# Dealing a gated linear recurrence and windowed attention out to four engines in a written order, with the first rows of the output projection among them

## The chip, the cores and the metric

The kernel runs on one core of a Trainium2 chip. Time is device microseconds of one execution, the median of several runs. The engines named below are TensorE (PE, with its weight loads as PEld), VectorE (DVE), ScalarE (ACT), GpSimd (POOL) and SyncE (SP), which here only starts DMAs. Each engine works through its own instructions in order and waits on semaphores for the others.

## The reference

One layer of a decoder trunk on 1024 tokens of width 1024. The normed input is projected to 30 columns of 128. They feed three mixers: HGRN2, a gated linear recurrence with 4 heads of 128; attention over three dilated windows, 4 heads of 64, combined by their softmax denominators; and RWKV-7. Their outputs, side by side, go through an output projection; a gated MLP with a short convolution and a per-layer embedding follow.

```python
z = rmsnorm(h, norm_mix_g[l]) @ w_in[l]
o_a = hgrn2_mix(a_q, a_f, a_i, a_g, lbs[l], hgrn_gnorm_g[l])   # this stage
o_b = dilated_window_mix(b_q, b_k, b_v)                        # this stage
o_c, v_first = rwkv7_mix(c_in, ...)                            # done before it
h = h + concatenate([o_a, o_b, o_c], -1) @ w_out[l]            # the stage behind it
h = h + conv_glu_ffn(rmsnorm(h, norm_ffn_g[l]), ...)
gate = sigmoid(rmsnorm(h, norm_ple_g[l]) @ ple_gate[l])
h = h + gate * (p[l] @ ple_proj[l])
# hgrn2, per head: S_t = diag(f_t) S_{t-1} + (1 - f_t) i_t^T, o_t = S_t^T q_t, then
# o * rsqrt(mean(o*o) + eps) * gnorm_g * silu(g)
```

## The kernel before

Tiles hold 128 rows (a column of the projection, or 128 features) by T = 1024 tokens, in two halves of HT = 512. A projection product is done in split precision: a weight is cut into a high part `whi` and a low part `wlo`, an input into `xh` and `xl`, and three matmuls of 128x512 stand for one (lines 130, 132, 134). ACT casts `whi` (line 106), DVE or POOL subtracts to get `wlo` (line 108). The raw weights `wraw` have two buffers.

The kernel runs in stages: input norm, projection and RWKV-7 (0 to about 434 us of the profile), the stage with HGRN2 and attention (about 434 to 646), the output projection (to about 730), the MLP and the rest. The change is in the third part of `phase_mix`. There four generators are interleaved, each a stream of steps that end in `yield`:

- A does HGRN heads 0 and 2, B heads 1 and 3 (`hgrn_head`). A head loads `f` and `q` (tiles `zl`), makes the key `hk` and `qt`, and goes through one step with key-query products `hsc` at line 1002 and seven steps at line 1023. A step copies `hsc` into the score tile `hS` under a mask (line 1025), multiplies `hk` (1026, on POOL and DVE by turns) and `qt` (1028), makes the next level of decays `hT` (1033) and the next packed key `ks` (ACT, 1013). Then come transposes (`vt`, with copies `hV`, `hkt` on ACT), the chunk states `hkv` and `hst`, the output `hpo` and its copy `ho`, and a norm: square `hsq` on ACT, sum `hss` on DVE, power `hrs` on POOL, multiply `ho` on DVE (1100), transposes `vt` on PE (1106).
- C does attention for two head pairs p, each over query blocks qb 0 to 9 (`swa`): scores `swq` (1167), a masked copy with a row minimum `lg` on DVE (1174), the exponential on ACT (1176), transposes `swt` (1190) with copies `pT`, values `swo` (1203) with copies `ob`, and at the end denominators `swd` and the division. A step of C does scores of qb, values of qb-2 and transposes of qb-1 together.
- F projects the three columns of `w_in` that were left over (`project_late`), a half of 24 matmuls `zp` per step; the result is scaled by `rstd` on DVE (306), goes through a sigmoid on ACT (472) and a multiply (474) into `zst`, and is stored to memory as a column `z`.

`interleave` calls the streams by the letters of `order`: 36 rounds with one step of A each, from round 6 one of B, one of C in 23 of them, one of F in the odd rounds up to 13. This is the order in which the code is written; the order on each engine is then made by the tile scheduler, from its own cost model and priorities. PSUM has a pool of four banks (`mx`) for the small products and two double banks (`dp`) shared by the scores `swq` and the dense products `dp`.

Of the kernel before, what the change touches and what calls it, by code (L numbers as in the profile page):

```python
# [10 lines left out]
F32 = mybir.dt.float32  # L11
# [7 lines left out]
P = 128  # L19
# [48 lines left out]
def interleave(order, streams):  # L68

    live = dict(streams)  # L70
    while live:
        for s in order:
            if s in live and next(live[s], STOP) is STOP:
                del live[s]
# [5 lines left out]
class Trunk:  # L80
# [227 lines left out]
    def phase_mix(self):  # L308
        nc, tc = self.nc, self.tc
        self.mix_norm()  # L310
        with tc.tile_pool(name="slots", bufs=1) as slots:
            self.slots, self.NSLOT = slots, 8
            self.rwkv()
        self.O, self.done = None, []
        for p in (0, 1):
            self.o_split(6 + p)
        with tc.tile_pool(name="hg", bufs=1) as slots, tc.tile_pool(name="sw", bufs=1) as sp:
            self.slots, self.NSLOT = slots, 11
            self.hgrn_setup()
            self.sp = sp  # L320
            self.swmask = sp.tile([P, T], F32, name="swmask")
            nc.scalar.dma_start(self.swmask, self.a["swm"])
            A = chain(self.hgrn_head(0), self.hgrn_head(2))
            B = chain(self.hgrn_head(1), self.hgrn_head(3))
            order = []
            for r in range(36):
                order += "C" * (r in self.TURNS) + "A" + "B" * (r > 5) + "F" * (r % 2 and r < 14)
            interleave(order, {"A": A, "B": B, "C": self.swa(sp), "F": self.project_late(self.rest)})

    TURNS = [i * 33 // 22 for i in range(23)]  # L330

    def mix_norm(self):

# [140 lines left out]
            self.nc.vector.tensor_tensor(dst, dst, src, ALU.mult)  # L474

    def project_late(self, js):


        nc = self.nc
        for j in js:  # L480
            w = self.load_w(self.a["w_in"][j])
            t = self.keep.tile([P, T], F32, tag="zst", name=self.nm("zst"), bufs=2)
            d = self.zpool.tile([P, T], F32, tag=f"z{j}", name=f"z{j}")
            kind = (j - 8) % 4 if j < 24 else 2
            turn = j < 24 and kind < 3
            for hf in (0, 1):
                ps = self.mxp.tile([P, HT], F32, tag="mx", name=self.nm("zp"))
                self.dense({hf: ps}, w, self.X, ND, halves=(hf,))
                dst = slice((hf ^ turn) * HT, ((hf ^ turn) + 1) * HT)
                r = self.R[:, hf * HT:(hf + 1) * HT]  # L490
                self.finish(kind, t[:, dst], *((ps[:, ::-1], r[:, ::-1]) if turn and hf else (ps, r)))
                nc.sync.dma_start(d[:, dst], t[:, dst])
                if hf:
                    self.z[j] = d
                yield
        self.O = self.xall()
        for k in self.done:
            self.o_split(k)
# [472 lines left out]
    def hgrn_head(self, h):  # L971
# [71 lines left out]
        for hf in (0, 1):  # L1043
            pt = mxp.tile([P, HT], F32, tag="mx", name=self.nm("vt"))
            for c in range(4):
                nc.tensor.transpose(pt[:, c * P:(c + 1) * P], vc[:, hf * HT + c * P:hf * HT + (c + 1) * P], self.ident)
            nc.scalar.copy(V[:, hf * HT:(hf + 1) * HT], pt)
        kt = self.slot("hkt")
        for hf in (0, 1):
            pt = mxp.tile([P, HT], F32, tag="mx", name=self.nm("vt"))  # L1050
# [46 lines left out]
        rs = spool.tile([P, 8], F32, tag="hrs", name=self.nm("hrs"))  # L1097
        nc.gpsimd.tensor_tensor(rs, ss, self.mhalf[:, :8], ALU.pow)
        o3 = o.rearrange("p (c v) -> p c v", v=P)
        nc.vector.tensor_tensor(o3, o3, rs.unsqueeze(2).broadcast_to([P, 8, P]), ALU.mult)  # L1100
        yield
        for hf in (0, 1):
# [9 lines left out]

    def swa(self, sp):

        pend, fin, load = [], None, self.swa_load(sp, 0)
        yield
        for p in (0, 1):
            d = load
            self.swa_values_in(d)
            for qb in range(10):  # L1120
                if fin:
                    self.swa_out(*fin)
                    fin = None
                if qb < 8:
                    cur = self.swa_scores(sp, d, qb)
                if qb > 1:
                    fin = self.swa_values(sp, d, *pend.pop(0))
                if 0 < qb < 9:
                    pend[-1:] = [self.swa_turn(sp, *pend[-1])]
                if qb < 8:  # L1130
                    pend.append((qb, *cur))
                if qb == 7 and p == 0:
                    load = self.swa_load(sp, 1)
                yield
        self.swa_out(*fin)

    def swa_load(self, sp, p):
        d = {"p": p}
        for i, n in enumerate("qkv"):
            d[n] = self.zload(24 + 3 * p + i, lambda n: sp.tile([P, T], F32, tag="sslot", name=self.nm(n), bufs=4),  # L1140
                              self.nc.gpsimd)
        return d

    def swa_values_in(self, d):
        nc, vc = self.nc, d["v"]
        V = self.sp.tile([P, T], F32, tag="sslot", name=self.nm("sV"), bufs=4)
        for hf in (0, 1):
            pt = self.mxp.tile([P, HT], F32, tag="mx", name=self.nm("vt"))
            for c in range(4):
                nc.tensor.transpose(pt[:, c * P:(c + 1) * P], vc[:, hf * HT + c * P:hf * HT + (c + 1) * P], self.ident)  # L1150
            nc.scalar.copy(V[:, hf * HT:(hf + 1) * HT], pt)
        d["V"] = V.rearrange("p (b c) -> p b c", c=P)

# [74 lines left out]
    def phase_out(self, hp, x0, emb):  # L1228


        nc = self.nc
        self.h = [hp.tile([P, T], F32, name=f"h{k}") for k in range(ND)]
        self.hd = [[self.zpool.tile([P, HT], F32, tag=f"hd{k}_{hf}", name=f"hd{k}_{hf}") for hf in (0, 1)] for k in range(ND)]
        for k in range(ND):
            nc.scalar.dma_start(self.h[k], self.a["xT"][k])
        acc = hp.tile([P, HT], F32, name="acc")

        def rows(m, halves, hooks={}):
            w = self.load_w(self.a["w_out"][m])
            ps = self.dps.tile([P, T], F32, tag="dp", name=self.nm("dp"))  # L1240
            self.dense([ps[:, :HT], ps[:, HT:]], w, self.O, (6, 7, 0, 1, 4, 2, 3, 5), halves, hooks)
            for g in halves:
                u = self.h[m][:, g * HT:(g + 1) * HT]
                nc.vector.tensor_tensor(u, u, ps[:, g * HT:(g + 1) * HT], ALU.add)
                nc.scalar.dma_start(self.hd[m][g], u)

        for m in range(ND):
            rows(m, (0, 1) if m < 2 else (0,))
            self.sq_acc(acc, self.h[m][:, :HT], m == 0)
        r = {}  # L1250

        def factor(i):
            if i == 0:
                r[0] = self.rstd_sums(acc, 1.0 / 1024, EPS, self.mxp.tile([P, 4], F32, tag="mx", name=self.nm("ps_ss")))
            else:
                r[1] = self.rstd_spread(r[0], self.mxp.tile([P, HT], F32, tag="mx", name=self.nm("ps_ss")))

        with self.tc.manual_schedule(engines={mybir.EngineType.PE}):
            rows(2, (1,), {0: lambda: factor(0), 3: lambda: factor(1)})
        pb = r[1]  # L1260
        x0.close()
        self.TX = {}
        for i, n in enumerate(("p1", "p2")):
            self.TX[n] = [[self.tile16(8 * i + 2 * k + c, F32R) for c in (0, 1)] for k in range(4)]
        self.ped = [self.zpool.tile([P, T], F32, tag=f"pe{m}", name=f"pe{m}") for m in range(ND)]
        pwp = emb.enter_context(self.pool("pw"))
        px, pw = [], []
        parts = [(px, self.pxp, "pT", 0), (pw, pwp, "ple_proj", 0), (px, self.pxp, "pT", 1), (pw, pwp, "ple_proj", 1)]
        norm = self.ffn_norm(0, pb)
        for m in range(3, ND):  # L1270
            rows(m, (1,))
            for _ in range(2):
                next(norm, None)
            if parts:
                self.pe_load(pwp, *parts.pop(0))
        for m in range(ND):
            self.sq_acc(acc, self.h[m][:, HT:], m == 0)
# [575 lines left out]
```

## Time and profile before

| | us |
|---|---|
| median of 3 runs (1493.87 to 1499.34) | 1497.36 |
| the profiled execution | 1496.24 |
| its span | 1494.5 |
| PE busy | 1445.1 (97%) |
| DVE busy | 1097.8 (73%) |
| ACT busy | 634.5 (42%) |
| POOL busy | 446.6 (30%) |

The mean granted clock of PE is 0.989 over the span. Times within the profile are from the span's start. A matmul's end is modelled and neighbours overlap, so the distance between two starts is the better price of one. A row with a wait says which engine waited at which line, and for what; "idle before" in a group is the idle time of its engine just ahead of its instructions.

### The profile page before, as it was taken

What the parts mean: (1) busy time and instruction counts of PE and PEld (TensorE: products, weight loads), DVE (VectorE), ACT (ScalarE), POOL (GpSimd) and SP (SyncE); (2) the same over time, 40 slices, a digit from 0 to 9 for tenths busy, and PEclk for the clock granted to TensorE, in tenths of its full rate; (3) what the DMA queues carried; (4) which work ended last, traced back from release to release, by engine and by line L of the source; (5) the groups of instructions that cost most, each with busy time, mean ns of one, the idle gap of its engine ahead of it and who ended that gap; (6) DMA issues with size and microseconds to landing.
All of it is one profiled execution on the core that took longest, in us unless ns stands there. A gap on an engine that the chain in (4) does not pass through costs nothing.

```text
span 1494.5 us, 20176 instructions
## 1 busy us (share of the span) xinstructions
PE 1445.1 (97%) x7416; PEld 1199.0 (80%) x7416; DVE 1097.8 (73%) x1650; ACT 634.5 (42%) x1121; POOL 446.6 (30%) x362
## 2 busy tenths in 40 slices
PE   8999999999989889999999999999999999999996
PEld 7888997888977677778878888888888888888775
DVE  7666455585648668736788888888888799777684
ACT  6531343213425635425454444444444444455542
POOL 3232432313412122112144554444554000002343
PEclk9999999999999989999999999999999999999998
DMA  6123112232152111165333333333332883351443
GB/s 219 58 92 99 43 56 72 72 99 63 43 179 74 42 73 57 43 229 194 127 110 98 103 106 106 106 106 106 106 106 81 313 298 97 105 164 42 139 157 106
DMA packets 79874, 167.83 MB, mean 112 GB/s; under 512 B 20064, under 2 KB 22240, under 8 KB 79776
## 3 DMA queue, kind: packets, MB, share of 16 engines
q1 hardware_dynamic: 65424, 145.44, 29.8%
q10 hardware_dynamic: 13264, 17.04, 3.4%
q0 software_dynamic: 1088, 4.06, 0.8%
q8 instruction: 58, 0.95, 0.3%
q14 instruction: 40, 0.33, 0.1%
HBM read 120.12 MB, written 46.40 MB: 111 GB/s over the span
## 4 chain that ended last, share of the span: by engine, by line
PE 84%; DVE 6%; issue 4%; POOL 2%; DMA 2%; ACT 1%; DVEq 0%; POOLq 0%; ACTq 0%; SPq 0%
PE bg L1325 16%; PE bv L1325 12%; PE dp L130 8%; PE dp L134 8%; PE dp L132 8%; PE bg L1626 7%; PE bv L1626 7%; PE hsc L1023 2%; DMA zl<-z 1%; PE swq L1167 1%; PE swo L1203 1%; POOL wlo L108 1%; PE bv L130 1%; PE bv L132 1%; PE swt L1190 1%
## 5 line engine op out<-in xcount | busy, mean ns | idle before, releaser
L130 PE MATMUL dp<-xh,whi 128*128 128x512 f32 x560 | 202.7, 406 | 1.1 <-ACT xh L374 1.1
L134 PE MATMUL dp<-xh,wlo 128*128 128x512 f32 x560 | 194.4, 391 | 2.0 <-POOL wlo L108 1.1
L132 PE MATMUL dp<-xl,whi 128*128 128x512 f32 x560 | 194.5, 391 | 0.4 <-DVE xl L375 0.3
L108 POOL TENSOR_TENSOR wlo<-raw,whi 128x512 fp32r<-128x512 f32 x84 | 138.0, 1662 | 77.8 <-ACT whi L106 77.8
L108 POOL TENSOR_TENSOR wlo<-wraw,whi 128x512 fp32r<-128x512 f32 x64 | 88.0, 1379 | 233.2 <-ACT whi L106 203.9
L1325 PE MATMUL bg<-t,whi 128*128 128x512 f32 x352 | 132.7, 389 | 0.0
L106 ACT CAST whi<-wraw 128x512 fp32r<-128x512 f32 x120 | 72.1, 617 | 132.7 <-PE dp L132 94.4
L134 PEld LDWEIGHTS dp<-xh,wlo 128*128 128x128 f32 x560 | 105.0, 188 | 25.0 <-POOL wlo L108 1.5
L130 PEld LDWEIGHTS dp<-xh,whi 128*128 128x128 f32 x560 | 104.5, 188 | 23.6 <-issue 3.8
L132 PEld LDWEIGHTS dp<-xl,whi 128*128 128x128 f32 x560 | 105.2, 188 | 21.8 <-DVE xl L375 1.4
L108 POOL TENSOR_TENSOR wlo<-s,whi 128x512 fp32r<-128x512 f32 x44 | 65.9, 1498 | 159.5 <-ACT whi L106 147.3
L1626 PE MATMUL bg<-t,whi 128*128 128x512 f32 x308 | 95.0, 389 | 0.0
L1626 PE MATMUL bv<-t,whi 128*128 128x512 f32 x308 | 94.8, 389 | 0.0
L106 ACT CAST whi<-raw 128x512 fp32r<-128x512 f32 x88 | 52.6, 619 | 97.4 <-PE bv L1325 49.0
L106 ACT CAST whi<-s 128x512 fp32r<-128x512 f32 x66 | 38.9, 620 | 120.7 <-PE bg L1325 113.3
L1325 PEld LDWEIGHTS bg<-t,whi 128*128 128x128 f32 x352 | 66.0, 188 | 13.6
L175 POOL TENSOR_TENSOR rst<-rst,mhalf 128x4 f32<-128x4 f32 (+1 forms) x9 | 9.8, 1088 | 223.4 <-DVE rst L173 223.4
L108 DVE TENSOR_TENSOR wlo<-wraw,whi 128x512 fp32r<-128x512 f32 x56 | 48.2, 863 | 34.8 <-ACT whi L106 32.4
L1622 ACT CAST t<-t 128x512 fp32r<-128x512 f32 x77 | 47.8, 622 | 47.8 <-PE bv L1626 34.8
L1626 PEld LDWEIGHTS bv<-t,whi 128*128 128x128 f32 x308 | 57.8, 188 | 12.1
L1626 PEld LDWEIGHTS bg<-t,whi 128*128 128x128 f32 x308 | 57.7, 188 | 12.0
L1325 PE MATMUL bg<-t,wlo 128*128 128x512 f32 x176 | 67.2, 389 | 0.0
(429 smaller groups left out, 3660.9 us busy)
## 6 DMA issues: line engine op xcount, KB each, us to landing
raw<-in_ffn_up_dram SPq DMA_DIRECT2D x44, 512.0 KB, 3.7
wraw<-in_w_in_dram SPq DMA_DIRECT2D x29, 512.0 KB, 3.6
z<-zst SPq DMA_DIRECT2D x19, 512.0 KB, 2.9
gb<-ct SPq DMA_DIRECT2D x33, 256.0 KB, 2.0
t<-gb SPq DMA_DIRECT2D x33, 256.0 KB, 2.8
t<-gt SPq DMA_DIRECT2D x33, 256.0 KB, 2.7
zl<-z SPq DMA_DIRECT2D x16, 512.0 KB, 3.5
wraw<-in_ple_gate_dram SPq DMA_DIRECT2D x16, 512.0 KB, 3.6
```

Source lines behind the costliest of these rows:

```text
L106: nc.scalar.copy(hi, src)
L108: eng.tensor_tensor(lo, src, hi.bitcast(F32), ALU.subtract)
L130: nc.tensor.matmul(ps[hf], wh, xh[hf], start=first, stop=False)
L132: nc.tensor.matmul(ps[hf], wh, xl[hf], start=False, stop=False)
L134: nc.tensor.matmul(ps[hf], wl, xh[hf], start=False, stop=last)
L1023: nc.tensor.matmul(sc[:, c, :], ks[:, c * P:(c + 1) * P], view(qt, c * P, [2 * n, 64 // n], [HT + n, 2], [1, n]), start=True, stop=True)
L1167: nc.tensor.matmul(pq[h][:, b:b + w], d["q"][hs, qb * P:nk], d["k"][hs, b:b + w], start=True, stop=True)
L1190: nc.tensor.transpose(pt[:, kb * P:(kb + 1) * P], lg[:, b + kb * P:b + (kb + 1) * P], self.ident)
L1203: nc.tensor.matmul(po[hs, :], d["V"][:, kb, hs], pT[h][:, kb * P:(kb + 1) * P], start=kb == 0, stop=kb == qb)
L1325: nc.tensor.matmul(ps, w[part == 2][:, s], X[k][part == 1], start=start and k == part == 0, stop=k == 3 and part == 2, skip_group_check=no ...
L1622: nc.scalar.copy(xh, x)
L1626: nc.tensor.matmul(ps[m], wt[part == 2][:, m * P:(m + 1) * P], (xh, xl)[part == 1], start=k == part == 0, stop=k == NK - 1 and part == 2)
```

## The change

It has five parts.

1. The streams run under `manual_schedule` for PE, DVE, ACT and POOL: on these four engines the instructions stand as the code is written. SP is still put in order by the scheduler. The letters come from `mix_order`: 39 rounds; a table gives each step its PE time in arbitrary units, and a step of C is dealt to a round when the sum so far is below the round's share. F's seven steps stand in rounds 0, 1, 3, 5, 7, 9 and 10, so that two halves of 24 products run back to back at the start.
2. A new stream W does the first five of eight products (k = 6, 7, 0, 1, 4) of the output projection's rows m = 0 and 1, in rounds 33 to 38; `rows` then adds the last three.
3. A step of C becomes three (scores; values; transposes), and two more yields in a head put the sum `hss` with the power `hrs`, the multiply of `ho`, and the transposes into three rounds.
4. The attention loads no longer share four slots: each has a tag of its own. For the second pair, q goes to a buffer of another pool and k to the place of the first pair's v, both through SP's queue after qb 5; v goes to the place of the first q through POOL's queue after qb 7.
5. `project_late` loads each next weight one column ahead and splits it right behind the second half of the column before.

```diff
+            late = self.project_late(self.rest)
+            E = mybir.EngineType
+            with tc.manual_schedule(engines={E.PE, E.DVE, E.Activation, E.Pool}):
+                interleave(self.mix_order(), {"A": A, "B": B, "C": self.swa(sp), "F": late, "W": self.out_steps()})
+    def mix_order(self):
+        head = [0, 0, 16] + [8] * 7 + [8, 8, 14, 30, 0, 0, 8]
...
+        late = (0, 1, 3, 5, 7, 9, 10)
+        per = (2 * sum(pairs) + sum(swa) + 48 * 6) / 36
...
+            while swa and done < per * (r + 1):
+                done += swa.pop(0)
+                n += 1
+            order += "A" * (r < 33) + "C" * (n // 2) + "B" * (r > 5) + "C" * (n - n // 2) + "F" * (r in late)
+            order += "W" * {33: 1, 35: 1, 36: 3, 37: 3, 38: 3}.get(r, 0)
...
+    def out_steps(self):
+        raws = [self.load_raw(self.a["w_out"][m]) for m in (0, 1)]
+        yield
+        for m in (0, 1):
+            w = self.split_w(raws[m])
+            ps = self.dps.tile([P, T], F32, tag="dp", name=self.nm("dp"))
+            self.part[m] = w, ps
+            for k in self.OUT_KS[:5]:
+                self.mm3([ps[:, :HT], ps[:, HT:]], w(k), self.O[k], k == 6, False)
+                yield
...
+            if more:
+                raw = self.load_raw(self.a["w_in"][js[n + 1]])
...
                 if hf:
                     self.z[j] = d
+                    if more:
+                        w = self.split_w(raw)
                 yield
...
         nc.gpsimd.tensor_tensor(rs, ss, self.mhalf[:, :8], ALU.pow)
         o3 = o.rearrange("p (c v) -> p c v", v=P)
+        yield
         nc.vector.tensor_tensor(o3, o3, rs.unsqueeze(2).broadcast_to([P, 8, P]), ALU.mult)
         yield
...
                 if qb < 8:
                     cur = self.swa_scores(sp, d, qb)
+                yield
                 if qb > 1:
                     fin = self.swa_values(sp, d, *pend.pop(0))
+                if qb == 1:
+                    self.swa_values_in(d)
+                yield
                 if 0 < qb < 9:
                     pend[-1:] = [self.swa_turn(sp, *pend[-1])]
                 if qb < 8:
                     pend.append((qb, *cur))
-                if qb == 7 and p == 0:
-                    load = self.swa_load(sp, 1)
+                if p == 0 and qb == 5:
+                    self.swa_load(ds[1], self.keep, "q", "oc", 2, self.nc.sync)
+                    self.swa_load(ds[1], sp, "k", "sc", 1, self.nc.sync)
+                if p == 0 and qb == 7:
+                    self.swa_load(ds[1], sp, "v", "sa")
                 yield
...
+            if m in self.part:
+                w, ps = self.part.pop(m)
+                for k in self.OUT_KS[5:]:
+                    self.mm3([ps[:, :HT], ps[:, HT:]], w(k), self.O[k], False, k == 5)
```

Where the order on the engines changes, two places. First PE at the end of a half of the late projection, before the change. Names carry a number for each buffer written; a row is an instruction, or several alike.

```order
1698 L134 MATMUL zp_3905<-xh_119,wlo_3901 128x512
1699 L1203 MATMUL swo_3944<-pT_3861,sV_3704 64x128
1700 L1203 MATMUL swo_3944<-pT_3866,sV_3704 64x128
...
1703 L1190 MATMUL swt_3951<-cst,lg_3850 128x128 x3
1704 L1190 MATMUL swt_3957<-cst,lg_3853 128x128 x3
1705 L1023 MATMUL hsc_3962<-qt_3732,ks_3890 128x128 x4
1706 L1167 MATMUL swq_3978<-zl_3696,zl_3694 128x512
1707 L1167 MATMUL swq_3979<-zl_3696,zl_3694 128x512
...
```

With the change, at the end of the third half (the second is `zp_3753`):

```order
1686 L134 MATMUL zp_3854<-xh_119,wlo_3786 128x512
1687 L1070 MATMUL hsc_3883<-qt_3751,ks_3847 128x128 x4
1688 L1246 MATMUL swt_3895<-cst,lg_3810 128x128
1689 L1246 MATMUL swt_3899<-cst,lg_3813 128x128
1690 L1223 MATMUL swq_3902<-zl_3708,zl_3706 128x384
1691 L1223 MATMUL swq_3903<-zl_3708,zl_3706 128x384
1692 L1070 MATMUL hsc_3912<-qt_3751,ks_3891 128x128 x4
1693 L130 MATMUL zp_3923<-xh_89,whi_3780 128x512
```

Behind a half stood two lots of values, two of transposes, an `hsc` and the scores; now an `hsc`, two single transposes and the scores, and then the next `hsc`.

DVE at the same places, before:

```order
489 L1033 TENSOR_TENSOR hT_4071<-hT_4071 128x8
490 L306 TENSOR_TENSOR zp_3905<-zp_3905,rstd 128x512
491 L1025 COPY_PREDICATED hS_3773<-cmask,hsc_3962 128x512
492 L474 TENSOR_TENSOR zst_3903<-zst_3903,zp_3905 128x512
493 L1028 TENSOR_TENSOR qt_3732<-qt_3732,hT_3775 128x2x32x8
494 L1026 TENSOR_TENSOR hk_3729<-hk_3729,hT_3775 128x2x8x32
495 L1174 ISA lg_3984,sden_3977<-swq_3978,swmask 128x640
496 L1174 ISA sden_3977 128x1
```

and with the change:

```order
455 L1080 TENSOR_TENSOR hT_3790<-zl_3712 128x512
456 L306 TENSOR_TENSOR zp_3854<-zp_3854,rstd 128x512
457 L513 TENSOR_TENSOR zst_3852<-zst_3852,zp_3854 128x512
458 L1072 COPY_PREDICATED hS_3788<-cmask,hsc_3883 128x512
459 L1073 TENSOR_TENSOR hk_3748<-hk_3748,hT_3790 128x2x128x2
460 L1075 TENSOR_TENSOR qt_3751<-qt_3751,hT_3790 128x2x128x2
461 L1080 TENSOR_TENSOR hT_3790<-hT_3790 128x256
```

Before, the mask copy of `hsc` stands between the scaling of `zp` and its multiply into `zst`; now both stand ahead of the mask copy, and `hk` and `qt` behind it, with the levels `hT` each behind its `qt`. Lines of the new file stand 47 to 56 rows further down here: 1072 is 1025, 1075 is 1028, 1080 is 1033, 513 is 474, 1230 is 1174.

Second, the loads of the second attention pair. Before, all three are on POOL: q, `zl_4394`, early (row 121), k and v, `zl_4396` and `zl_4398`, here:

```order
133 L157 TENSOR_TENSOR xl_4507<-oc_1640,xh_4506 128x512
134 L108 TENSOR_TENSOR wlo_5630<-wraw_5622,whi_5628 128x512
135 L157 TENSOR_TENSOR xl_4509<-oc_3267,xh_4508 128x512
136 L502 DMA zl_4396<-z_3663 128x1024
137 L502 DMA zl_4398<-z_3745 128x1024
138 L1098 TENSOR_TENSOR hrs_4480<-hss_4477,mhalf 128x8
139 L1026 TENSOR_TENSOR hk_4024<-hk_4024,hT_4071 128x2x4x64
```

and `zl_4395` (k) and `zl_4393` (q) on SP with the change, among the loads of weights and of the other heads:

```order
70 L537 DMA z_3719<-zst_3718 128x512 x2
71 L97 DMA wraw_5346<-in_w_out_dram 128x1024
72 L549 DMA zl_4395<-z_3663 128x1024
73 L549 DMA zl_3976<-z_1168 128x1024
74 L549 DMA zl_3978<-z_1236 128x1024
75 L537 DMA z_3853<-zst_3852 128x512 x2
76 L97 DMA wraw_5348<-in_w_out_dram 128x1024
77 L549 DMA zl_4085<-z_1037 128x1024
78 L537 DMA z_4018<-zst_4017 128x512 x2
79 L549 DMA zl_4393<-z_3620 128x1024
```

The third of them, v, stays with POOL, as before. K's load now stands ahead of the loads of head 1 (`zl_3976`, `zl_3978`), q's ahead of the later loads of the heads.

More of the change, by code (lines that the diff above doesn't have):

```diff
@@ L324, in phase_mix @@
             B = chain(self.hgrn_head(1), self.hgrn_head(3))
[L325 to L330, printed above, removed]
+            self.part = {}
+            late = self.project_late(self.rest)
[4 more added lines that the diff above has]
+        head = [0, 0, 16] + [8] * 7 + [8, 8, 14, 30, 0, 0, 8]
+        pairs = head[:-1] + [head[-1] + head[0]] + head[1:]
+        swa = [0]
+        for _ in (0, 1):
+            for qb in range(10):
+                n = qb + 1
+                swa += [(3.5 * n if qb < 8 else 0) + 5 * (qb in (4, 8)), (2.6 * (n - 2) if qb > 1 else 0) + 8 * (qb == 1),
+                        2 * qb if 0 < qb < 9 else 0]
+        swa += [5]
+        late = (0, 1, 3, 5, 7, 9, 10)
+        per = (2 * sum(pairs) + sum(swa) + 48 * 6) / 36
+        order, done = ["C"], 0
+        swa.pop(0)
+        for r in range(39):
+            a = pairs[r] if r < len(pairs) else 0
+            b = pairs[r - 6] if r > 5 else 0
+            done += a + b + 48 * (r in late[:6])
+            n = 0
+            while swa and done < per * (r + 1):
[3 more added lines that the diff above has]
+            order += "W" * {33: 1, 35: 1, 36: 3, 37: 3, 38: 3}.get(r, 0)
+        return order + ["C"] * len(swa)
+    OUT_KS = (6, 7, 0, 1, 4, 2, 3, 5)
+    def out_steps(self):
[8 more added lines that the diff above has]
+                yield
     def mix_norm(self):
@@ L476, in project_late, with late_steps @@
     def project_late(self, js):
+        raw = self.load_raw(self.a["w_in"][js[0]])
+        return self.late_steps(js, self.split_w(raw))
+    def late_steps(self, js, w):
         nc = self.nc
-        for j in js:
-            w = self.load_w(self.a["w_in"][j])
+        for n, j in enumerate(js):
+            more = n + 1 < len(js)
+            if more:
+                raw = self.load_raw(self.a["w_in"][js[n + 1]])
             t = self.keep.tile([P, T], F32, tag="zst", name=self.nm("zst"), bufs=2)
@@ L1113, in swa @@
     def swa(self, sp):
-        pend, fin, load = [], None, self.swa_load(sp, 0)
+        pend, fin = [], None
+        ds = {0: {"p": 0}, 1: {"p": 1}}
+        self.swa_load(ds[0], sp, "q", "sa")
+        self.swa_load(ds[0], sp, "k", "sb")
+        self.swa_load(ds[0], sp, "v", "sc")
         yield
         for p in (0, 1):
-            d = load
-            self.swa_values_in(d)
+            d = ds[p]
             for qb in range(10):
@@ L1125, in swa @@
                     cur = self.swa_scores(sp, d, qb)
+                yield
                 if qb > 1:
                     fin = self.swa_values(sp, d, *pend.pop(0))
+                if qb == 1:
+                    self.swa_values_in(d)
+                yield
                 if 0 < qb < 9:
@@ L1131, in swa, with swa_load @@
                     pend.append((qb, *cur))
-                if qb == 7 and p == 0:
-                    load = self.swa_load(sp, 1)
+                if p == 0 and qb == 5:
[3 more added lines that the diff above has]
+                    self.swa_load(ds[1], sp, "v", "sa")
                 yield
         self.swa_out(*fin)
[L1137 to L1142, printed above, removed]
+    def swa_load(self, d, pool, n, tag, bufs=1, eng=None):
+        j = 24 + 3 * d["p"] + "qkv".index(n)
+        d[n] = self.zload(j, lambda n: pool.tile([P, T], F32, tag=tag, name=self.nm(n), bufs=bufs), eng or self.nc.gpsimd)
     def swa_values_in(self, d):
         nc, vc = self.nc, d["v"]
-        V = self.sp.tile([P, T], F32, tag="sslot", name=self.nm("sV"), bufs=4)
+        V = self.sp.tile([P, T], F32, tag="sd", name=self.nm("sV"), bufs=1)
         for hf in (0, 1):
@@ L1238, in rows @@
         def rows(m, halves, hooks={}):
-            w = self.load_w(self.a["w_out"][m])
-            ps = self.dps.tile([P, T], F32, tag="dp", name=self.nm("dp"))
-            self.dense([ps[:, :HT], ps[:, HT:]], w, self.O, (6, 7, 0, 1, 4, 2, 3, 5), halves, hooks)
+            if m in self.part:
+                w, ps = self.part.pop(m)
+                for k in self.OUT_KS[5:]:
+                    self.mm3([ps[:, :HT], ps[:, HT:]], w(k), self.O[k], False, k == 5)
+            else:
+                w = self.load_w(self.a["w_out"][m])
+                ps = self.dps.tile([P, T], F32, tag="dp", name=self.nm("dp"))
+                self.dense([ps[:, :HT], ps[:, HT:]], w, self.O, self.OUT_KS, halves, hooks)
             for g in halves:
```

## The prediction

> **What bounds the kernel now.** First I read busy time by stretch. The columns are the stretch, its length, then busy us and instruction count of PE, PEld, DVE, ACT and POOL, the granted PE clock, the DMA share and GB/s.
>
> ```profile
> 100.00:430.00 330.00, 328.31 (x1894) 281.94 (x1893) 201.38 (x401) 97.98 (x245) 101.77 (x114) 1.00 0.25 75
> 430.00:645.00 215.00, 190.43 (x1357) 153.62 (x1356) 149.22 (x286) 105.26 (x206) 45.35 (x38) 0.95 0.21 69
> 780.00:1440.00 660.00, 658.01 (x2914) 544.49 (x2913) 562.64 (x684) 299.66 (x451) 217.19 (x142) 1.00 0.39 127
> ```
>
> TensorE bounds everything, and it is full except in the stage that the change rewrites: there it idles 215.0 - 190.4 = 24.6 us and runs at a mean clock of 0.95. DVE, at 149 of 215, is second there. The waits of PE in this stage, by what ended them (total us, times, longest):
>
> ```profile
> PE vt L1106 <- DVE ho L1100: 8.0, 3, 4.4
> PE swq L1167 <- DMA zl<-z: 5.3, 1, 5.3
> PE hsc L1002 <- DVE hk L984: 3.7, 1, 3.7
> PE hsc L1023 <- DVE qt L1028: 3.4, 4, 1.6
> ...
> PE hsc L1023 <- DVE zst L469: 0.3, 1, 0.3
> ```
>
> Eleven kinds in all; the three big ones are 17.0 us. The chain of waits (start, us, what) says what stands behind each: a load of the first head, a load of the second attention pair, and the norm of a head's output on POOL and DVE.
>
> ```profile
> 435.38 7.63 DMA zl<-z
> ...
> 518.30 6.58 DMA zl<-z
> ...
> 538.11 2.16 POOL hrs L1098
> ...
> 540.30 2.08 DVE ho L1100
> 542.51 1.94 PE vt L1106 x8
> ```
>
> Idle time costs a second time through the clock. Cut into pieces of 3.41 us:
>
> ```profile
> 571.90:575.31 3.41, 1.52 (x6) 0.68 (x5) 2.29 (x6) 1.19 (x3) 1.64 (x1) 1.00 0.00 0
> 575.31:578.72 3.41, 3.39 (x18) 2.75 (x19) 3.31 (x6) 0.27 (x1) 0.00 (x0) 0.50 0.08 14
> 445.60:449.01 3.41, 3.41 (x18) 3.41 (x18) 1.96 (x5) 0.41 (x2) 0.22 (x1) 0.50 0.99 315
> 524.11:530.93 6.82, 5.57 (x24) 4.66 (x25) 1.05 (x6) 0.88 (x4) 0.00 (x0) 0.50 0.25 102
> 541.17:548.00 6.83, 5.49 (x34) 5.29 (x36) 5.71 (x8) 1.24 (x2) 1.85 (x3) 0.50 0.01 2
> ```
>
> A piece with PE busy 1.52 of 3.41 us is followed by one at clock 0.50. Six such pieces hold 3.39 + 3.41 + 5.57 + 5.49 = 17.9 us of half-speed work, which at full speed takes 8.9 us less. So 24.6 + 8.9 = 33.5 us are to be had at most, all in this stage.
>
> **The change part by part.** Durations that the sums need, first as PE ran them without a gap behind one projection half (start, us, instruction), then as groups (busy, mean ns, idle):
>
> ```profile
> 435.48 0.40 PE L132 MATMUL zp<-xl,whi 128*128 128x512 f32 x1
> 435.71 0.39 PE L134 MATMUL zp<-xh,wlo 128*128 128x512 f32 x1
> ...
> 468.48 0.66 PE L1203 MATMUL swo<-pT,sV 128*64 128x128 f32 x8
> 469.07 0.88 PE L1190 MATMUL swt<-cst,lg 128*128 128x128 f32 x6
> 469.78 1.06 PE L1023 MATMUL hsc<-qt,ks 128*128 128x128 f32 x8
> 470.77 1.35 PE L1167 MATMUL swq<-zl,zl 64*128 64x512 f32 x8
> 472.05 0.99 PE L1203 MATMUL swo<-pT,sV 128*64 128x128 f32 x12
> 472.97 1.09 PE L1190 MATMUL swt<-cst,lg 128*128 128x128 f32 x8
> 473.89 1.06 PE L1023 MATMUL hsc<-qt,ks 128*128 128x128 f32 x8
> ```
> ```profile
> L1025 DVE COPY_PREDICATED hS<-cmask,hsc 128x512 f32<-128x512 uint8 x28 | 20.6, 736 | 17.9 <-PE hsc L1023 17.6
> L1028 DVE TENSOR_TENSOR qt<-qt,hT 128x512 f32<-128x512 f32 x24 | 18.9, 788 | 0.0
> L1026 DVE TENSOR_TENSOR hk<-hk,hT 128x512 f32<-128x512 f32 x12 | 8.2, 681 | 0.1
> L1095 DVE TENSOR_REDUCE hss<-hsq 128x8 f32<-128x1024 f32 x4 | 4.9, 1215 | 5.2 <-ACT hsq L1093 5.2
> L1174 DVE CUSTOM_DVE_ANT_0 lg<-swq,swmask 128x768 f32<-128x768 f32 x4 | 3.7, 956 | 0.0
> L1040 DVE COPY_PREDICATED hS<-cmask,few 128x512 f32<-128x512 uint8 x4 | 3.7, 915 | 0.0
> L1039 DVE COPY_PREDICATED hS<-cmask,hS 128x512 f32<-128x512 uint8 x4 | 2.9, 729 | 0.0
> L306 DVE TENSOR_TENSOR zp<-zp,rstd 128x512 f32<-128x512 f32 x4 | 2.8, 697 | 5.6 <-PE zp L134 5.6
> L474 DVE TENSOR_TENSOR zst<-zst,zp 128x512 f32<-128x512 f32 x4 | 2.7, 677 | 0.0
> L108 DVE TENSOR_TENSOR wlo<-wraw,whi 128x512 fp32r<-128x512 f32 x3 | 2.1, 691 | 0.2 <-ACT whi L106 0.2
> L472 ACT ACTIVATE zst<-zp 128x512 f32<-128x512 f32 x4 | 2.4, 599 | 0.0
> L106 ACT CAST whi<-wraw 128x512 fp32r<-128x512 f32 x7 | 4.3, 619 | 11.1 <-PE zp L132 6.3 <-PE dp L132 4.8
> L1089 ACT COPY ho<-hpo 128x512 f32<-128x512 f32 x8 | 4.7, 587 | 12.3 <-PE hpo L1088 12.3
> ```
>
> Removed. The start: one zp product follows the other after 0.23 us, so a half of 24 is 5.5 us. Two halves now run ahead of the first hsc where one did, and 5.5 us of cover exceed the wait of 3.7 us: gone. The attention load: in the old order k, the second of the pair's loads, takes one of four shared slots on POOL's queue, once the first pair has left it; now q and k have buffers that are free early, and stand on SP at qb 5 with the scores of qb 6 and 7 and more between. The load takes 6.6 us, and a written round is about 6 us of PE: 5.3 us gone. On SP's queue these loads stand ahead of the second head's f and q, but the buffer that k waits for is free after round 2 and the head starts in round 6. The norm: hss, the ho multiply and the transposes now stand three rounds apart. Behind head 0's last hpo, PE has 768 and 896 wide scores, two hsc, 16 swo, 10 swt and the swd, some 8.2 us by the rows above (the scores scaled from 1.35 for 640 columns); the chain is ho copy 0.6, square about 1.1, hss 1.2, 0.2, then DVE's queue of two 768-wide lg (2.0), copy 0.7, hk 0.7, qt 0.8, 0.6 of small ones and the multiply (1.4 at its shortest), 9.4 us in all. POOL's hrs (2.2) fits within. So 1.2 us of the 4.4 stay, and of the two of 1.8 none. The small waits (7.3) are replaced by those counted next. All 24.6 us of idle time and 8.9 of clock are thus taken off: -33.5.
>
> Added, first: the written order on DVE. Behind each late half DVE must do zp times rstd (0.70), wait for the sigmoid on ACT (0.60), multiply (0.68), and only then copy hsc (0.74), hk (0.68) and qt (0.79) for the next hsc: 4.19 us. PE has meanwhile hsc 1.06, 2 swt 0.29, and a 384-wide pair of scores, about 0.8: 2.1. The old order had the seven rows quoted from 468.48 to 473.89 there and no gap. Three more halves, worked alike: cover 1.06 + 2 swo + 4 swt + a 512-wide pair (some 2.8) against 4.88 (a wlo of 0.69 comes in), 2.1; cover of one hsc and the other head's two (some 2.6) against 4.19, 1.6; cover of two vt pairs, hsc and 4 swo (3.6) against 5.8 (the mask copies of lines 1039 and 1040 come in, 0.73 and 0.92), 2.2. Sum 8.0; taken 7, since DVE issues the next instruction some 0.08 us before the end of the last. Bounds 4 and 8.
>
> Second: rounds in which DVE has more than PE. Adding such durations over the instructions of each round, DVE exceeds PE by 2.4 in rounds 14 and 15, 3.5 in 22 and 23, 2.2 in 28: 8.1, and 10.2 with all smaller excesses. Each stands between rounds where PE has more (13, 16, 21, 24, 27, 29), and a part of DVE's work isn't asked for before the next round. Taken 6; bounds 2 and 10.
>
> Third: stream W. Its ten products of six matmuls come out of the output projection that follows, so their 60 x 0.23 = 13.7 us are moved, not added, and they cover the last head's norm. But the split of w_out stands on ACT behind the two ho copies: 2 x 0.59 + 0.62 after the last hpo, less what PE still has, at most 2.0 us; taken 1.5, bounds 0 and 2. Its raw loads take SP's queue early and find their buffers free after rounds 1 and 3. The yields cost nothing themselves.
>
> Fourth: the clock. The one row with a wait of under 3 us before a half-speed piece is 571.90 above, with 1.9 idle in it. My waits of 1.6 to 2.2 lie just there, so some of them cost a piece, 1.7 us each. Six of the eight or so could; I take three, 5.1; bounds 0 and 14. [...]
>
> Sum: -33.5 + 1.2 + 7 + 6 + 1.5 + 5.1 = -12.7. The profiled execution took 1496.24 us (span 1494.5), 1.1 under the median of the runs, 1497.36. So the median should come to 1484.7; I say 1485. With all low ends: -33.5 + 1.2 + 6 = -26.3, 1471. With all high ends: -33.5 + 1.2 + 8 + 10 + 2 + 14 = +1.7, 1499.
>
> **The rivals.** (a) Nearly all is had: DVE catches up, waits fall to the low ends: 1471. For it: in the stretch 430 to 645 DVE is at 149 of 215, so on the mean it has room. Against: the room isn't where the late halves are. (b) The written order gives back what it takes. Waits in every dense round and behind every half at their high ends and four half-speed pieces (6.8): -33.5 + 1.2 + 8 + 10 + 2 + 6.8 = -5.5, 1492, which is no change. For it: four in-order engines that wait for each other; DVE's idle time before hsc's mask copy is 17.9 us now, so PE and DVE already take turns. (c) Slower, by one mechanism: the order on DVE and PE makes each round a barrier and each such wait falls into a piece of its own. Then 21.2 us of waits (1.2 + 8 + 10 + 2) stand against the 24.6 that went, and thirteen of them (four halves, eight dense rounds, W) draw a half-speed piece of 1.7, 22.1 us: +9.8, 1507. It decides from 33.5 us of new waits and pieces together, which is above the high ends of my bounds. (d) The moved loads come no sooner: SP runs its queue in order, and should k's load stall it, head 1's f and q come late: the 5.3 us and two pieces (3.4) remain, 1485 + 8.7 = 1494. Against it: the buffer is free four rounds before the head needs them.
>
> **How the numbers follow.** What a measurement can tell from no change is about 0.5%, 7.5 us: below 1489.9 is faster, above 1504.9 slower. Forecast (1478 to 1490) 0.40, (a) 0.18, (b) 0.20, (d) 0.07, (c) 0.15. Faster 0.58, same 0.27, slower 0.15. The likeliest, 1485, has 1478 to 1490 as its own range. For 8 in 10 the range must reach through (a), (b) and (d) and leaves out most of (c) and the last of (a): 1470 to 1504.
>
> **What would show it.** After: no wait of a swq on a DMA and no wait of the first hsc over 1 us; vt waiting for ho once, for 1 to 2 us; new waits of 1.5 to 2.5 us of hsc on DVE qt or hk, or on ACT ks, behind the second to fifth late projection halves, and in the rounds after them; fewer than six half-speed pieces; dp products ahead of the last vt. The forecast is wrong if the stage's idle time stays above 24 us, if its clock stays at 0.95 or below, or if one load still stops PE.

## The result, and the profile after

The changed kernel takes 1506.02 us, the median of 7 runs (1504.94 to 1507.94), against 1497.36 before: 1.006 times as long, 95% interval 1.0045 to 1.0074. The forecast was 1485 (1470 to 1504). The change makes the kernel slower by 0.6%, just outside the range. The profiled execution has a span of 1503.2 us against 1494.5; at 1504.94 us it is the fastest of the 7.

Busy time by stretch, after (columns as before):

```profile
100.00:430.00 330.00, 328.50 (x1896) 282.24 (x1895) 201.27 (x400) 97.33 (x244) 101.33 (x114) 1.00 0.24 73
430.00:645.00 215.00, 186.43 (x1339) 150.48 (x1338) 149.06 (x286) 100.75 (x205) 42.69 (x36) 0.94 0.19 64
780.00:1440.00 660.00, 656.83 (x2901) 543.43 (x2900) 558.66 (x680) 297.32 (x446) 216.77 (x142) 1.00 0.39 127
```

The place is the right one: PE is nearly as full in the other two stretches as it was, and the stage idles more (28.6 us of 215, before 24.6) at a lower clock (0.94, before 0.95). Between the same two points, the last product ahead of the stage and the norm behind the output projection, the two profiles read:

```profile
432.89:737.58 304.69, 279.12 (x1757) 226.41 (x1756) 202.56 (x364) 142.92 (x270) 65.51 (x54) 0.97 0.32 109
```
```profile
432.62:745.18 312.56, 280.49 (x1757) 227.74 (x1756) 205.15 (x366) 139.01 (x269) 64.27 (x52) 0.96 0.32 108
```

The first is before, the second after: 7.9 us of the 8.7 by which the spans differ, with the same 1757 matmuls, of which 6.5 are idle time (25.6 to 32.1) and 1.4 are matmuls that run longer. The waits of PE in this stretch, after:

```profile
PE hsc L1070 <- ACT ks L1060: 5.3, 3, 2.0
PE dp L130 <- ACT whi L106: 4.5, 2, 2.8
PE swo L1259 <- ACT pT L1247: 3.4, 3, 1.8
PE hsc L1049 <- ACT hkt L1101: 3.0, 1, 3.0
PE swt L1246 <- ACT hkt L1101: 2.4, 2, 1.4
PE hsc L1070 <- DVE hT L1080: 2.4, 2, 2.1
...
PE swt L1246 <- ACT ob L1260: 1.5, 2, 0.8
...
PE swt L1246 <- ACT lg L1232: 1.4, 1, 1.4
PE vt L1155 <- DVE ho L1149: 1.1, 1, 1.1
PE vt L1093 <- ACT pT L1247: 1.1, 1, 1.1
```

None of the three big waits of before is left at its size: no swq waits for a load, the first hsc for no hk, and vt for ho 1.1 us instead of 8.0. In their place stand seventeen kinds of small ones, 31.5 us, and ACT is named in 22.8 of these, which it hardly was before. Two of them, as they look on ACT and DVE. Behind the first of the four late halves (start, us, instruction, and in brackets the idle time before it):

```profile
456.90 0.60 ACT L511 ACTIVATE zst<-zp 128x512 f32<-128x512 f32 x1 [4.21 <-DVE zp L306]
459.54 0.62 ACT L1060 COPY ks<-hk 128x512 f32<-128x512 f32 x1 [2.04 <-DVE hk L1073]
```
```profile
456.17 0.70 DVE L306 TENSOR_TENSOR zp<-zp,rstd 128x512 f32<-128x512 f32 x1 [3.55 <-PE zp L134]
457.53 0.69 DVE L513 TENSOR_TENSOR zst<-zst,zp 128x512 f32<-128x512 f32 x1 [0.66 <-ACT zst L511]
458.14 0.72 DVE L1072 COPY_PREDICATED hS<-cmask,hsc 128x512 f32<-128x512 uint8 x1
458.75 0.68 DVE L1073 TENSOR_TENSOR hk<-hk,hT 128x512 f32<-128x512 f32 x1
```

DVE waits 0.66 us for the sigmoid, with the mask copy, hk and the key copy ks behind it; PE waits 2.05 us at 460.21. ACT is named there only because ks is the last link. The other kind stands in ACT's queue; first the transposes on PE whose results the copies hkt are to take, then ACT:

```profile
534.22 1.09 PE L1100 MATMUL vt<-cst,hk 128*128 128x128 f32 x8
```
```profile
537.91 1.15 ACT L1232 ACTIVATE lg<-lg,sden 128x1024 f32<-128x1024 f32 x1 [5.06 <-DVE sden L1230]
539.06 1.14 ACT L1232 ACTIVATE lg<-lg,sden 128x1024 f32<-128x1024 f32 x1
540.20 1.05 ACT L1101 COPY hkt<-vt 128x512 f32<-128x512 f32 x2
```

ACT idles 5.06 us for DVE's scores, then does two exponentials, and only then the copies hkt, which could have been made from 535.3 on and whose PSUM banks PE needs: a wait of 2.96 us at 540.82. DVE's order has a part in this: from 534.00 to 536.65 it prepares the next head (zl, hk, qt), and only then takes the scores. The clock, in pieces of 3.41 us:

```profile
469.65:473.07 3.42, 1.31 (x8) 0.49 (x5) 3.42 (x8) 1.16 (x4) 0.76 (x2) 1.00 0.59 182
473.07:476.48 3.41, 3.41 (x12) 2.84 (x12) 2.96 (x9) 3.38 (x7) 1.17 (x2) 0.52 0.50 202
500.38:507.20 6.82, 6.12 (x23) 4.14 (x24) 5.30 (x8) 4.36 (x9) 3.58 (x3) 0.51 0.25 80
541.34:544.75 3.41, 3.41 (x19) 3.41 (x18) 1.37 (x3) 1.30 (x3) 2.07 (x2) 0.52 0.02 5
561.82:565.23 3.41, 3.41 (x28) 3.08 (x24) 0.18 (x2) 0.27 (x1) 0.00 (x0) 0.52 0.00 0
575.47:578.89 3.42, 3.42 (x12) 1.43 (x11) 3.08 (x6) 2.05 (x7) 0.00 (x0) 0.52 0.00 0
640.32:643.74 3.42, 3.42 (x9) 2.63 (x10) 1.64 (x3) 0.60 (x2) 2.49 (x2) 0.52 0.50 153
674.46:677.87 3.41, 3.41 (x10) 2.63 (x9) 0.69 (x1) 0.36 (x1) 0.14 (x1) 0.52 0.80 219
```

Eight half-speed pieces instead of six (the row from 500.38 is two), seven in the stage and one behind it. One more stands far behind, from 1418.56, where the kernel before has none.

### The profile page after: what moved, and what is told of

The parts are those of the page before. It is cut to its first block, busy times and chain, and to the rows that moved or that the text cites. A ratio compares the mean times of both kernels' runs of the same rounds, so it can differ in the third digit from the quotient of the medians.

```text
span 1503.2 us, 20180 instructions
## 1 busy us (share of the span) xinstructions
PE 1447.7 (96%) x7416; PEld 1201.1 (80%) x7416; DVE 1100.0 (73%) x1650; ACT 629.3 (42%) x1119; POOL 445.2 (30%) x360
## 4 chain that ended last, share of the span: by engine, by line
PE 84%; DVE 6%; issue 4%; ACT 3%; POOL 2%; DMA 1%; DVEq 0%; ACTq 0%; POOLq 0%
PE bg L1386 16%; PE bv L1386 11%; PE dp L130 8%; PE dp L134 8%; PE dp L132 8%; PE bg L1687 7%; PE bv L1687 7%; PE hsc L1070 1%; POOL wlo L108 1%; PE swq L1223 1%; PE zp L134 1%; PE zp L130 1%; PE zp L132 1%; PE bv L130 1%; PE bv L134 1%
## 5 line engine op out<-in xcount | busy, mean ns | idle before, releaser
L108 DVE TENSOR_TENSOR wlo<-wraw,whi 128x512 fp32r<-128x512 f32 x56 | 51.6, 924 | 39.3 <-ACT whi L106 36.5
```

The costliest lines, as they stand in the source:

```text
L108: eng.tensor_tensor(lo, src, hi.bitcast(F32), ALU.subtract)
```

## The experiments

The theory after the first look: the order as written costs, on ACT above all (theory A) and on DVE behind the late halves (theory B). Rivals: PE's own written order (theory C), or stream W and the loads. Each ratio is against the kernel before, on the same chip. In the five sets of runs the kernel before took 1497.2 to 1498.6 us, so medians of different sets compare to about 1.4 us.

**Which engine's order costs.** Four kernels differ from the changed one only in the set of engines that keep the written order. PE's order is the same, instruction for instruction, wherever PE is in the set.

```diff
-            with tc.manual_schedule(engines={E.PE, E.DVE, E.Activation, E.Pool}):
+            with tc.manual_schedule(engines={E.PE, E.DVE, E.Pool}):          # no_act
+            with tc.manual_schedule(engines={E.PE, E.Activation, E.Pool}):   # no_dve
+            with tc.manual_schedule(engines={E.PE}):                         # pe_only
+            if True:                                                         # sched_all
```

ACT freed:

> The changed kernel, with ScalarE left to the scheduler and PE, DVE and POOL in the written order as before. Theory A (ScalarE's written order costs most: exponentials stand ahead of the copies hkt and pT on which PE waits, 12 to 13 us of the new waits and three or four half-speed pieces): about 1488 to 1494, and no wait of hsc or swt on hkt. Theory B (DVE's written order costs most: the finish of a late half stands ahead of the next mask copy): 1502 to 1506, with the four waits behind the late halves unchanged at 1.5 to 2.1 each. Theory C (PE's own order is what costs): 1502 to 1506, the waits moving to other engines.

1492.7 us, ratio 0.9963 (0.9948 to 0.9977): 13 us better than the change, inside theory A's forecast. Its waits in the same stretch:

```profile
PE hsc L1070 <- ACT ks L1060: 8.2, 4, 2.6
...
PE hsc L1070 <- DVE hT L1080: 1.8, 2, 1.6
...
PE swt L1246 <- ACT hkt L1101: 0.6, 1, 0.6
```

The waits on hkt fall from 5.4 to 0.6, as the scheduler puts these copies ahead of the exponentials. The half-speed pieces in this stretch fall from eight to two. Theory A has the time right with other shares: the waits of the stretch fall by 7.0 us (31.5 to 24.5), not 12 to 13, and six half-speed pieces go, not three or four. The waits on ks behind the late halves are all still there, though they name ACT: their cause isn't ACT's order.

DVE freed:

> The changed kernel with VectorE left to the scheduler and PE, ACT and POOL in the written order. ScalarE freed alone took 13 us away, VectorE and POOL freed on top of it 8.5. If the two costs stand apart: 1496 to 1499, with the four waits behind the late halves (8.1 us) down to 2 or less, and the waits on hkt still there. If VectorE's freedom is worth something only where ScalarE follows: 1502 to 1506, the late halves' waits unchanged.

1498.44, ratio 1.0008 (0.9996 to 1.0021), 7.6 better than the change, as forecast for costs that stand apart. The waits behind the late halves shrink to one of 0.43 us,

```profile
PE hsc L1070 <- DVE qt L1075: 0.7, 2, 0.4
PE hsc L1049 <- ACT hkt L1101: 1.1, 1, 1.1
```

so theory B holds for that place. The costs don't stand quite apart: the waits on hkt, which were to stay, fall from 5.4 to 2.1. Now the state sums hst come late (6.1 us in three waits).

Both and POOL freed:

> The changed kernel, with only PE in the written order and DVE, ACT and POOL left to the scheduler. Theories A and B together: 1480 to 1490, the waits behind late halves and those on hkt and pT mostly gone. Theory C: still 1500 to 1506, since PE asks for results sooner than any order of the others can give them.

1484.18, ratio 0.9906 (0.9887 to 0.9926). 13.3 and 7.6 make 20.9; together they are worth 21.8. PE's order, with the others free, is 13 us faster than before: theory C is not the main cost. POOL was freed only together with the others, so its own share is not known.

All freed:

> The changed kernel without the manual order on any of the four engines in this stage; streams, loads, yields and stream W as changed. If the manual order is the whole loss (A, B or C): below 1497, about 1485 to 1495, since the loads' stall of 5.3 us stays away. If other parts (W, the loads, the prefetch of weights) cost: 1500 or more.

1477.4, ratio 0.9862 (0.9841 to 0.9884), better than the best expected. So theory C holds in part, with 6.8 us, and the manual order as a whole costs 28.6 of the 1506.0. The stage, with the scheduler:

```profile
430.00:645.00 215.00, 206.31 (x1451) 164.54 (x1450) 160.34 (x302) 107.27 (x213) 47.01 (x38) 1.00 0.29 102
```

8.7 us idle, clock 1.00, and 112 matmuls more done by 645 than in the changed kernel. At the same late half DVE now runs:

```profile
449.71 0.68 DVE L1073 TENSOR_TENSOR hk<-hk,hT 128x512 f32<-128x512 f32 x1
...
455.79 1.76 DVE L1080 TENSOR_TENSOR hT<-hT 128x8 f32<-128x8 f32 x7
457.47 0.69 DVE L306 TENSOR_TENSOR zp<-zp,rstd 128x512 f32<-128x512 f32 x1
458.07 0.72 DVE L1072 COPY_PREDICATED hS<-cmask,hsc 128x512 f32<-128x512 uint8 x1
458.68 0.68 DVE L1075 TENSOR_TENSOR qt<-qt,hT 128x512 f32<-128x512 f32 x1
459.28 0.55 DVE L1230 CUSTOM_DVE_ANT_0 lg<-swq,swmask 128x384 f32<-128x384 f32 x1
459.75 0.55 DVE L1230 CUSTOM_DVE_ANT_0 lg<-swq,swmask 128x384 f32<-128x384 f32 x1
460.23 0.68 DVE L513 TENSOR_TENSOR zst<-zst,zp 128x512 f32<-128x512 f32 x1
```

The sigmoid's time is filled, the multiply stands four instructions later, and hk is not in the chain at all: it was done at 449.71, ahead of the projection half, and levels hT up to 457.47 during it, while the changed kernel's DVE idled for 3.55 us. PE waits 0.62 there.

**Can the written order be mended by hand.** First the late halves: the finish behind the next step of A.

```diff
                 self.dense({hf: ps}, w, self.X, ND, halves=(hf,))
+                yield
...
-            order += "A" * (r < 33) + "C" * (n // 2)
+            order += "A" * (r < 33) + "F" * (r - 1 in late[:6]) + "C" * (n // 2)
```

> The changed kernel, all four engines in the written order, but the finish of a late projection half (scaling, sigmoid, multiply) written behind the next step of A instead of ahead of it. Theory B for this place: the four waits of 1.5 to 2.1 behind the late halves, 7.5 us, shrink to about 1 each and two or three half-speed pieces go: 1496 to 1501. Rival: the finish meets another step there, and DVE's load decides, not its order: 1504 to 1507.

1506.87, ratio 1.0061 (1.0042 to 1.008): nothing. The time is the rival's, but its reason is not shown: with the same load on DVE, no_dve has these waits all but gone. The waits behind the late halves move one step on and change their names:

```profile
474.94 1.16 PE L1071 MATMUL hsc<-qt,ks 128*128 128x128 f32 x8 [2.41 <-DVE zst L513]
...
487.31 1.55 PE L1071 MATMUL hsc<-qt,ks 128*128 128x128 f32 x8 [1.57 <-DVE zst L513]
...
499.07 1.16 PE L1071 MATMUL hsc<-qt,ks 128*128 128x128 f32 x8 [1.26 <-ACT ks L1061]
```

DVE's wait for the sigmoid is longer, 1.10, 1.30, 1.35 and 1.34 us instead of 0.66: on ACT a table load of 1.28 us now stands right ahead of the first three of these sigmoids, where the changed kernel had it done ahead (from 464.06 for the one at 467.60), and two copies hV ahead of the fourth. And hk and hT still stand among the mask copies and qt. So the move brought a cost of its own, and the run does not price the order alone. By my reading, what the scheduler does and one moved step does not is to interleave single instructions of several steps.

Then ACT: the exponentials one step of C later.

```diff
-            nc.scalar.activation(lg[:, :nk], lg[:, :nk], AF.Exp, bias=nm, scale=-1.0, ...)
+            self.exps.append((lg[:, :nk], nm, den[:, 2 * qi + h:2 * qi + h + 1]))
...
                 yield
+                for lg, nm, acc in self.exps:
+                    self.nc.scalar.activation(lg, lg, AF.Exp, bias=nm, scale=-1.0, accum_out=acc)
```

> The changed kernel, all four engines in the written order, but the exponentials of a block written one step of C later, behind the copies of the heads' next steps (another table load or two may come in on ScalarE). If what costs is that the exponentials stand ahead of hkt and ob: the waits on hkt (5.4 us) go and three of the half-speed pieces with them, 1495 to 1501. Rival: ScalarE is then late with pT and lg, and the waits of swo and swt grow by as much: 1504 to 1512.

1507.1, ratio 1.0059 (1.0038 to 1.0079): again the rival. The waits on hkt do go (0.5 us), and others take their place:

```profile
PE swt L1249 <- ACT ob L1263: 3.1, 3, 2.7
...
PE swt L1249 <- DVE pT L1250: 2.0, 1, 2.0
```

The half-speed pieces of the stretch rise from eight to nine. So theory A is right on where the time goes (no_act), but not that one kind of instruction in the wrong place is all of it.

**Stream W.**

```diff
-                interleave(self.mix_order(), {..., "F": late, "W": self.out_steps()})
+                interleave(self.mix_order(), {..., "F": late})
```

> The changed kernel without stream W: the output projection's first two rows are done whole in the stage behind. Theory that W costs: the wait of 1.7 us at its start and that of 2.8 us in the output projection on whi go, 1500 to 1503. Theory that W pays, by covering the norm of the last head: a wait of vt on ho of 2 to 5 us and a half-speed piece come in, 1506 to 1511.

1500.0, ratio 1.0015 (1.0002 to 1.0027), 6 better than the change: W costs in the written order. Its start wait of 1.7 goes and vt waits 0.9 more, which does not make up 6. The wait on whi behind the stage, which I had put down to W, stays at 2.3 of 2.8. Not all of the 6 us is accounted for; the profile has one half-speed piece less (1.7).

> The scheduler on all four engines, all of the change except the manual order and stream W. If W covers the last head's norm under the scheduler too: 1480 to 1485, with a wait of vt on ho at the end. If the scheduler fills that place from the output projection by itself, as in the kernel before: 1474 to 1478, without the wait of 2.8 us on whi behind W's rows.

1474.03, ratio 0.9838 (0.9818 to 0.9858), beside 0.9862 (0.9841 to 0.9884) with W: the intervals overlap, so no gain of W is shown under the scheduler. Without it vt waits 1.7 us for ho, and the wait on whi is gone.

> The scheduler on all four engines with W, and the weights of the output projection's row 3 split ahead of row 2's products, so that ScalarE's casts no longer stand behind the square of row 2. The wait of 2.8 us on whi and the half-speed piece behind it (1.7) go: 1472 to 1474. Rival: the casts then delay something else by as much: 1476 to 1479.

```diff
+                w = early.pop(m, None) or self.load_w(self.a["w_out"][m])
+                if m == 2 and 0 in halves:
+                    early[3] = self.load_w(self.a["w_out"][3])
```

1472.28, ratio 0.9833 (0.9812 to 0.9853). Expected against sched_all was 3 to 5 less; the medians differ by 5.1, but the intervals overlap. In the profile the wait of 2.84 on whi is gone, in its place stands one of 1.5 on wlo (0.3 in sched_all), and the half-speed pieces that sched_all had from 643.4, 756.1 and 1390.9 us are gone too; only the first of the three stands behind that wait. This and sched_no_w are the fastest versions run, 1.7% and 1.6% faster than before, and not to be told apart.

**Where the good parts of the change are.** The loads alone, on the kernel before:

> The kernel before, with only the attention loads changed (buffers of their own, q and k of the second pair on SP at block 5, v on POOL at block 7). The stall of swq on the load, 5.3 us and two half-speed pieces, goes: 1488 to 1492. Rival: the scheduler moves the work up and the time comes back as a wait of another kind: 1495 to 1499.

1489.77, ratio 0.9941 (0.9919 to 0.9964), as expected: the wait for the load falls from 5.3 to 1.3 us, and the half-speed pieces of the stretch from six to four. The wait of the first hsc on hk falls too, from 3.7 to 1.8, which I hadn't expected and which stays unexplained.

```profile
PE vt L1106 <- DVE ho L1100: 8.0, 3, 4.4
PE hsc L1023 <- DVE qt L1028: 3.4, 4, 1.6
PE hsc L1002 <- DVE hk L984: 1.8, 1, 1.8
PE swq L1171 <- DMA zl<-z: 1.3, 1, 1.3
```

The two yields in a head, taken out of sched_no_w. Only one of them is in the norm, ahead of the multiply of ho; the other, unlike what part 3 of the change says, stands between the transposes for hV and those for hkt:

> The scheduler on all four engines without W, and without the two yields in a head. If the yields are what took the waits of vt on ho away: these come back, 4 to 8 us with one to three half-speed pieces, 1480 to 1487 against 1474. If attention in three steps is enough for that: 1472 to 1476.

1486.92, ratio 0.9924 (0.9904 to 0.9945): 13 us worse than with them, at the upper end of what was expected. The waits on ho are back, with two half-speed pieces in the stretch where sched_no_w has none. Which of the two yields pays is not shown.

```profile
PE vt L1153 <- DVE ho L1147: 6.1, 4, 2.6
PE hsc L1070 <- DVE qt L1075: 4.0, 3, 1.6
```

And stream F in its old rounds:

> The scheduler on all four engines without W, and stream F in rounds 1, 3, 5, ... as before instead of two halves first. If the first head's load needs the cover of two halves: a wait of the first hsc on hk of 2 to 4 us and a half-speed piece, 1477 to 1481. If the scheduler brings the second half forward by itself: 1472 to 1476.

1476.8, ratio 0.9852 (0.9828 to 0.9876) against 0.9838: not told apart, and between the two expectations. No wait on hk comes back, but not because a second half came forward. The scheduler puts attention work there, scores, values and transposes from 435.14 to 442.95, then one late half, and the first hsc at 448.53. So the first head's load needs cover, but here attention work gives it as well as a second half.

## Why the prediction was wrong, point by point

- *The bound, the place, and what would go*: right, with luck in one number. The stretch holds 7.9 of the 8.7 us, and the three big waits went: 3.7 and 5.3 to none, 8.0 to 1.1, where I had worked out 1.2 (the rows of that chain add up to 9.3, not 9.4). But those 1.2 were to stay at head 0's norm, whose transposes at 526.03 wait for nothing; the 1.1 stand at 617.90 at head 2's, which had no such wait before.
- *The late halves*: right in mechanism and size. Forecast 2.1, 2.1, 1.6 and 2.2; measured 2.05, 2.11, 1.47 and 1.82, 7.5 where I took 7.
- *The rounds in which DVE has more than PE*: this is the step that failed. I took 6, with bounds 2 and 10. The rest of the stage's waits, without the late halves (7.5), the norm (1.1), W's start (1.9) and those behind the stage (3.5), are 31.5 - 14.0 = 17.5 us. Some 13 of them name ACT (hkt 5.4, pT 4.7, ob 1.5, lg 1.4). I had added DVE's load per round, and gave ACT's queue in these rounds no term and no reason for that. But ACT's queue in the written order waits for DVE's scores with ready copies behind it: ahead of the row at 537.91 it idled 5.06 us. With ACT freed (no_act) these 13 us fall to 3.6, and six half-speed pieces go with them: 13 us of time. Some of it is DVE's order too, since the waits on hkt also fall in no_dve.
- *Stream W*: half right. The start wait was 1.7 on whi where I took 1.5, and the last vt no longer waits. That it costs nothing else was wrong, by some 5 us in the written order. The wait of 2.84 on whi behind the stage was not foreseen at all; but it stays at 2.3 without W, so W is not its cause in the written order.
- *The clock*: right in kind, mis-sized. I took three new half-speed pieces, 5.1 us, with a bound of 14, which is eight pieces, though I held six for possible (10.2). Eight were there, and they hold 26.6 us of half-speed work (before had 17.9), which at full speed takes 13.3 us less, where I took 5.1. They came behind short waits: the longest of the stage was 2.96 us, and in the piece ahead of 473.07 PE was busy for 1.31 of 3.42 us.
- *The sum*: -33.5 of idle time and clock against +31.5 of waits and 26.6 / 2 = 13.3 of clock is +11.3, where I had -12.7. Most of the miss is in three places: the rounds (17.5 for 6), the clock (13.3 for 5.1) and the waits behind the stage (3.5 for nothing). The stretch grew by only 7.9. Of the 3.4 us between, 3.0 are the clock's: 8.7 us more of half-speed work should make the matmuls 4.4 us longer, and they took 1.4 longer. Why is open.
- *The signs*: of those I had named, the stage's idle time (28.6 us, above 24), its clock (0.94) and the half-speed pieces (eight, not fewer than six) went against me.
- *The rivals*: (c), slower, gave 1507 and came nearest, but not by its own sum: it had 21 us of waits, nearly all DVE's, and 22 of clock; measured were 31.5 and 13.3, and that the two sums are close is luck. (d) fell, since no load stopped PE. That DVE has room on the mean, the argument for (a), is no evidence in a fixed order: with all four engines freed, PE is busy for 206 of 215.

## What to carry to other kernels

The written order on several engines was here a chain of waits in which an engine's head instruction held back ready work behind it: ACT idled 5.06 us for DVE's scores, while the copies hkt behind it could have been made from 535.3 on. Before pinning an engine, look at its queue for instructions that wait for another engine (an exponential for scores, a multiply for a sigmoid) and at what PE needs from behind them, also on an engine that is half idle. Pin engines one at a time and time each: here the same streams, steps and loads were 1.4% faster under the scheduler and 0.6% slower pinned.

## What was not expected of the hardware

Half-speed pieces came behind short waits, and not behind all of them: a wait of 2.05 us at 460.21 drew none, one of 1.71 at 638.81 did. In the changed kernel's stretch the starts at 500.38, 541.34, 561.82, 575.47, 640.32 and 674.46 lie 8, 20, 26, 30, 49 and 59 times 3.413 us behind that at 473.07 (these starts are some 0.1 us early: the clock falls at 473.2, and the rows read 0.52 where 473.19 to 476.60 reads 0.50). In the 3.41 us ahead of each of these seven PE was idle for 1.7 to 2.9 us, in one wait or several (ahead of 575.47, 1.40 and 0.54 us); the eighth followed a half-speed piece. What draws a piece is not shown: of two neighbours, the piece from 667.63 with PE busy 1.64 of 3.42 us drew none, that from 671.05 with 1.69 did, and so did the one from 1415.15 with 2.25. A piece of 3.41 us at half the clock does 1.7 us less work, so a part of a gain or loss of a few us can lie in how many pieces a version has; that is an estimate from these rows.
